# A two-layer decoder trunk on one core: GpSimd's instructions in the order in which the program emits them

## The chip, the cores and the metric

The kernel runs on one core of a Trainium2 chip. The metric is the device time of one execution in microseconds, lower is better; before the change it was run three times. The profile shows one further execution of the same program.

## The reference

Two layers, each with x of 512 tokens by 1024 channels, all in float32:

```
h = rms_norm(x) ; proj = h @ w_in[l]
pool_u, rq, rk, rv, rg, xq, gates = split(proj)
y_pool = pool_mixer(pool_u) ; y_ret = retention(rq, rk, rv, rg) ; y_mem = memory_attention(xq, rms_norm(mem))
merged = sum over branches of sigmoid(gate_b) * (y_b @ w_up_b)
x = x + merged @ w_out[l]
x = x + square(relu(rms_norm(x) @ w_mlp1[l])) @ w_mlp2[l]     # 1024 -> 4096 -> 1024
```

After the two layers a last rms_norm is returned.

## The kernel before, in words

A float32 product is made of float32r parts: `split` and `split_w` turn a tile into a high part (a ScalarE cast, L104 for operands, L114 for weights) and a low part (a VectorE subtraction, L105 and L117), and `mm` (L120 to L125) issues three matmuls, high by high (L123), high by low and low by high.

Most weights are multiplied as a `Weight`: a block of 1024 by 1024 in four quarters q00, q01, q10, q11, and seven products in the order 1, 2, 5, 3, 6, 4, 7, instead of eight. A weight has three raw operands of two tiles each (kp = 0 and 1, 512 KB a tile), loaded by the SyncE queue (L200): A from q00, C from q10, B from q11. Each tile serves several products, because the sums are formed in place by accumulating transfers that GpSimd issues (`take`, L222 on), always after the split of the value that is replaced:

- product 1 splits A, then A += q01 (L236, from DRAM); product 5 splits that, then A += q11 (L236); product 6 splits that, with nothing added.
- product 3 splits B, then B += q01 (L236); product 7 splits that.
- product 2 splits C; when product 6 has split A, C += A (L238, from SBUF to SBUF); product 4 splits that.

In the text A0 and A1 are A's tiles for kp 0 and 1, and likewise B0, B1, C0 and C1. `skip` (L217 to L219) does the first of these sums for a weight whose product 1 was made ahead from a separate copy (`early`). So GpSimd has eight transfers for a weight, emitted as A0, A1 (+q01), A0, A1 (+q11), B0, B1, C0, C1:

```
            raw = self.buf[part][kp]
            wp = split_w(raw, between)
            if then is not None:
                nc.gpsimd.dma_start(raw, rows2(then, kp), accum_op=ALU.add)
            if p == 6:
                nc.gpsimd.dma_start(self.buf["C"][kp], raw, accum_op=ALU.add)
```

GpSimd has one other task: the power -1/2 of each norm's mean square (`rstd`, L555 to L557): `r` for the norms over a layer's rows, `yss` for the four token blocks of a retention head pair, `mr` for the memory's norm.

The operand of a product (`Operand`) has its own sums and splits x1 to x7; for a weight whose operand was used before they are there already, for the first weight of an operand they are made beside the weight's splits.

Splits are prepared ahead of their products: `push` (L176) queues a product with its preparation, and `prepare` runs the preparations of the LOOK = 3 products ahead (2 for product 4). Per layer the weights follow one another like this: five projection weights (retention values; retention queries and keys; the gates of three branches), the memory's keys and values (a `Plain` weight without products of sums), the retention gate, memory queries with pool channels, three `Plain` weights for the branches, w_out, then for each of four blocks the MLP's first (w_mlp1) and second product (w_mlp2). The second products add into x.

Two things decide the order of the instructions on an engine. For engines named in `MANUAL` (L37, handed to `tc.manual_schedule` at L78) it is the order in which the program emits them; that is TensorE. For all others a scheduler chooses an order from the dependences and priorities before the kernel runs; once chosen, it is fixed. The transfers of SyncE's queue, too, are in such an order.

Of the kernel before, what the change touches and what calls it, by code (L numbers as in the profile page):

```python
# [16 lines left out]
ET = mybir.EngineType  # L17
# [16 lines left out]
MAGIC = 12582912.0  # L34
NSLOT = 72
LOOK = 3
MANUAL = {ET.PE}  # L37


C_CNT = 0  # L40
# [28 lines left out]
def tile_trunk(ctx, tc, a, out):  # L69
# [7 lines left out]
    psum = ctx.enter_context(tc.tile_pool(name="psum", bufs=8, space=PSUM))  # L77
    ctx.enter_context(tc.manual_schedule(engines=MANUAL))  # L78

# [1218 lines left out]
```

## Time and profile before

| | us |
|---|---|
| three runs | 1693.96, 1690.39, 1689.86 |
| median | 1690.39 |
| the profiled execution, its own time | 1696.11 |
| its span, first to last instruction | 1694.4 |
| TensorE busy | 1619.8 (96%) |
| VectorE busy | 1263.5 (75%) |
| ScalarE busy | 1034.9 (61%) |
| GpSimd busy | 313.5 (19%) |

PE is TensorE, DVE VectorE, ACT ScalarE, POOL GpSimd. The busy share says how much of the span an engine computed; for GpSimd it holds the issuing of its transfers, not their flight. The granted clock of TensorE was 0.983 of full speed on average. In the rows, "idle before <-releaser" is the time for which an engine stood still before an instruction, and what ended that. A transfer that adds into a raw tile reads as raw<-in_w_... (from DRAM) or raw<-raw (L238).

### The profile page before, as it was taken

The numbers are of one execution on the slowest core, as the hardware profiler recorded it, in microseconds if no ns is written. First come the engines' busy times: TensorE is split into PE (matmuls) and PEld (weight loads), VectorE is DVE, ScalarE is ACT, GpSimd is POOL, SyncE is SP. The second block draws the span as 40 slices with busy tenths as digits, with TensorE's granted clock in tenths as the row PEclk, the third lists the DMA queues.
The fourth block names the chain that finished last, engine by engine and source line by source line (L and its number), as shares of the span: only waits on it lengthen the run. The fifth ranks groups of instructions, "written<-read, shape, count | busy, mean of one in ns | idle before, by whom it ended". The sixth has DMA issues, their size and how long they took to land. (4 is left out here: it accounts for less than half of the span.)

```text
span 1694.4 us, 24933 instructions
## 1 busy us (share of the span) xinstructions
PE 1619.8 (96%) x9396; PEld 1425.3 (84%) x9396; DVE 1263.5 (75%) x1727; ACT 1034.9 (61%) x1655; POOL 313.5 (19%) x292
## 2 busy tenths in 40 slices
PE   8899999999989899999989999999999889999997
PEld 7697888998879788989768888889878688989895
DVE  4787575767687788696966876757767778796868
ACT  6456676556357656475765577755544577566565
POOL 2122212200012222222231223022000212222221
PEclk9999999999999899999999999999999999999999
DMA  8699986873666788988887999678435769788775
GB/s 237 148 237 234 252 217 142 186 223 118 181 137 133 153 198 178 213 179 202 183 182 162 234 248 243 217 169 175 158 125 159 173 153 192 189 181 185 174 151 123
DMA packets 155256, 311.16 MB, mean 184 GB/s; under 512 B 11320, under 2 KB 12544, under 8 KB 155136
## 3 DMA queue, kind: packets, MB, share of 16 engines
q0 software_dynamic: 61440, 134.23, 46.3%
q1 hardware_dynamic: 83872, 159.42, 27.5%
q10 hardware_dynamic: 9824, 15.93, 2.6%
q8 instruction: 73, 1.20, 0.3%
q14 instruction: 47, 0.39, 0.1%
HBM read 255.01 MB, written 16.78 MB: 160 GB/s over the span
## 5 line engine op out<-in xcount | busy, mean ns | idle before, releaser
L117 DVE TENSOR_TENSOR wl<-raw,wh 128x1024 fp32r<-128x1024 f32 x496 | 603.7, 1221 | 291.4 <-ACT wh L114 282.0
L114 ACT CAST wh<-raw 128x1024 fp32r<-128x1024 f32 x496 | 519.5, 1051 | 487.7 <-PE P L125 126.6
L236 POOL DMA_DIRECT2D raw<-in_w_mlp x92 | 121.6, 1349 | 391.8 <-DVE wl L117 270.9
L236 POOL DMA_DIRECT2D raw<-in_w_in x80 | 104.9, 1371 | 355.1 <-DVE wl L117 209.9
L238 POOL DMA_DIRECT2D raw<-raw x64 | 57.6, 900 | 167.9 <-DMA raw<-in_w_in 68.6
L1184 DVE TENSOR_TENSOR x<-x,P 128x512 f32<-128x512 f32 x120 | 78.4, 679 | 5.1 <-PE P L125 4.9
L123 PE MATMUL P<-wh,x3h 128*128 128x512 f32 x160 | 64.4, 403 | 11.3 <-ACT x3h L104 11.3
L123 PE MATMUL P<-wh,x6h 128*128 128x512 f32 x160 | 64.6, 404 | 9.8 <-ACT x6h L104 6.5
L125 PE MATMUL P<-wh,x6l 128*128 128x512 f32 x160 | 64.4, 402 | 4.2 <-DVE x6l L105 4.2
L123 PE MATMUL P<-x6h,wh 128*128 128x256 f32 x192 | 56.6, 295 | 10.7 <-ACT P L368 10.7
L236 POOL DMA_DIRECT2D raw<-in_w_out x12 | 15.9, 1461 | 274.4 <-DVE wl L117 156.6
L125 PE MATMUL P<-wh,x5l 128*128 128x512 f32 x160 | 63.5, 397 | 2.8 <-DVE x5l L105 2.8
L123 PE MATMUL P<-wh,x5h 128*128 128x512 f32 x160 | 63.3, 396 | 2.0 <-ACT x5h L104 1.9
L124 PE MATMUL P<-wl,x4h 128*128 128x512 f32 x160 | 62.7, 392 | 2.3 <-DVE wl L117 2.3
L125 PE MATMUL P<-wh,x3l 128*128 128x512 f32 x160 | 64.3, 402 | 0.1
L124 PE MATMUL P<-wl,x6h 128*128 128x512 f32 x160 | 63.9, 399 | 0.0
L123 PE MATMUL P<-wh,x7h 128*128 128x512 f32 x160 | 63.5, 397 | 0.3
L124 PE MATMUL P<-wl,x3h 128*128 128x512 f32 x160 | 63.7, 398 | 0.0
L123 PE MATMUL P<-wh,x4h 128*128 128x512 f32 x160 | 62.8, 393 | 0.5 <-ACT wh L114 0.5
L123 PE MATMUL P<-wh,x1h 128*128 128x512 f32 x160 | 63.1, 395 | 0.0
L124 PE MATMUL P<-wl,x7h 128*128 128x512 f32 x160 | 62.6, 391 | 0.0
L124 PE MATMUL P<-wl,x1h 128*128 128x512 f32 x160 | 62.6, 391 | 0.0
(314 smaller groups left out, 5213.4 us busy)
## 6 DMA issues: line engine op xcount, KB each, us to landing
raw<-in_w_mlp SPq DMA_DIRECT2D x100, 512.0 KB, 5.0
raw<-in_w_mlp POOLq DMA_DIRECT2D x96, 512.0 KB, 7.3
raw<-in_w_in SPq DMA_DIRECT2D x88, 512.0 KB, 5.3
raw<-in_w_in POOLq DMA_DIRECT2D x84, 512.0 KB, 7.6
raw<-raw POOLq DMA_DIRECT2D x64, 512.0 KB, 6.7
sgl<-sig SPq DMA_DIRECT2D x48, 256.0 KB, 6.0
sig<-c ACTq DMA_DIRECT2D x36, 256.0 KB, 5.6
raw<-in_w_mem_kv SPq DMA_DIRECT2D x16, 512.0 KB, 5.4
```

Of the source, the lines that this page charges most:

```text
L114: nc.scalar.copy(hi, raw)
L117: nc.vector.tensor_tensor(lw, raw, hi.bitcast(F32), ALU.subtract)
L123: nc.tensor.matmul(ps, sh, mh, start=start, stop=False, skip_group_check=True)
L124: nc.tensor.matmul(ps, sh, ml, start=False, stop=False, skip_group_check=True)
L125: nc.tensor.matmul(ps, sl, mh, start=False, stop=stop, skip_group_check=True)
L236: nc.gpsimd.dma_start(raw, rows2(then, kp), accum_op=ALU.add)
L238: nc.gpsimd.dma_start(self.buf["C"][kp], raw, accum_op=ALU.add)
L1184: nc.vector.tensor_tensor(x, x, part, op)
```

## The change

GpSimd joins the engines whose instructions stay in the order of emission. How far ahead the splits are prepared (LOOK) stays as it was.

```
 NSLOT = 72
 LOOK = 3
-MANUAL = {ET.PE}
+MANUAL = {ET.PE, ET.Pool}
```

TensorE's and SyncE's instructions stand in the same order as before; GpSimd's change all along the program; ScalarE's and VectorE's change only at the borders of stages, as the scheduler that still orders them sees another GpSimd.

In the second product of the MLP's block 1 in layer 0, GpSimd's order was this (raw_6069 and raw_6071 are A0 and A1, raw_6383 and raw_6385 B0 and B1, raw_6255 and raw_6257 C0 and C1):

```order
L236 DMA raw_6069<-in_w_mlp2 128x2x512
L236 DMA raw_6071<-in_w_mlp2 128x2x512
L236 DMA raw_6069<-in_w_mlp2 128x2x512
L236 DMA raw_6071<-in_w_mlp2 128x2x512
L238 DMA raw_6255<-raw_6069 128x1024
L236 DMA raw_6383<-in_w_mlp2 128x2x512
L238 DMA raw_6257<-raw_6071 128x1024
L236 DMA raw_6385<-in_w_mlp2 128x2x512
```

and is this now:

```order
L236 DMA raw_6069<-in_w_mlp2 128x2x512
L236 DMA raw_6071<-in_w_mlp2 128x2x512
L236 DMA raw_6069<-in_w_mlp2 128x2x512
L236 DMA raw_6071<-in_w_mlp2 128x2x512
L236 DMA raw_6383<-in_w_mlp2 128x2x512
L236 DMA raw_6385<-in_w_mlp2 128x2x512
L238 DMA raw_6255<-raw_6069 128x1024
L238 DMA raw_6257<-raw_6071 128x1024
```

Both of B's sums moved ahead of both of C's.

At the start of layer 1, with its first projection weight (raw_8133 and raw_8135 are A0 and A1, raw_8407 and raw_8409 B0 and B1, raw_8317 and raw_8319 C0 and C1; raw_8609 and raw_8611 are the next weight's A0 and A1), GpSimd's order was:

```order
L236 DMA raw_8133<-in_w_in 128x2x512
L557 TENSOR_TENSOR r_8381<-r_8381,nhalf_90 128x2
L236 DMA raw_8135<-in_w_in 128x2x512
L219 DMA raw_8609<-in_w_in 128x2x512
L557 TENSOR_TENSOR r_8507<-r_8507,nhalf_90 128x2
L219 DMA raw_8611<-in_w_in 128x2x512
L236 DMA raw_8133<-in_w_in 128x2x512
L238 DMA raw_8317<-raw_8133 128x1024
L236 DMA raw_8135<-in_w_in 128x2x512
L236 DMA raw_8407<-in_w_in 128x2x512
L238 DMA raw_8319<-raw_8135 128x1024
L236 DMA raw_8409<-in_w_in 128x2x512
```

and is now:

```order
L557 TENSOR_TENSOR r_8381<-r_8381,nhalf_90 128x2
L236 DMA raw_8133<-in_w_in 128x2x512
L236 DMA raw_8135<-in_w_in 128x2x512
L557 TENSOR_TENSOR r_8507<-r_8507,nhalf_90 128x2
L236 DMA raw_8133<-in_w_in 128x2x512
L236 DMA raw_8135<-in_w_in 128x2x512
L236 DMA raw_8407<-in_w_in 128x2x512
L236 DMA raw_8409<-in_w_in 128x2x512
L238 DMA raw_8317<-raw_8133 128x1024
L238 DMA raw_8319<-raw_8135 128x1024
L219 DMA raw_8609<-in_w_in 128x2x512
L219 DMA raw_8611<-in_w_in 128x2x512
```

The power of the first half's factors moved to the front, the next weight's skip sums to the end, and C0's sum no longer stands ahead of A1's second one.

In the last gate weight of layer 0 (C0 and C1 are raw_1765 and raw_1767, B0 and B1 raw_1869 and raw_1871) and at the start of the retention gate's weight (A0 and A1 are raw_2475 and raw_2477) it was:

```order
L238 DMA raw_1765<-raw_1565 128x1024
L238 DMA raw_1767<-raw_1567 128x1024
L236 DMA raw_1869<-in_w_in 128x2x512
L236 DMA raw_1871<-in_w_in 128x2x512
L557 TENSOR_TENSOR mr_2119<-mr_2119,nhalf_90 128x1
L557 TENSOR_TENSOR mr_2182<-mr_2182,nhalf_90 128x1
L236 DMA raw_2475<-in_w_in 128x2x512
L557 TENSOR_TENSOR yss_2674<-yss_2674,nhalf_90 128x2
L236 DMA raw_2477<-in_w_in 128x2x512
L557 TENSOR_TENSOR yss_2724<-yss_2724,nhalf_90 128x2
L557 TENSOR_TENSOR yss_2776<-yss_2776,nhalf_90 128x2
L557 TENSOR_TENSOR yss_2810<-yss_2810,nhalf_90 128x2
```

and is now:

```order
L236 DMA raw_1869<-in_w_in 128x2x512
L557 TENSOR_TENSOR mr_2119<-mr_2119,nhalf_90 128x1
L236 DMA raw_1871<-in_w_in 128x2x512
L238 DMA raw_1765<-raw_1565 128x1024
L557 TENSOR_TENSOR mr_2182<-mr_2182,nhalf_90 128x1
L238 DMA raw_1767<-raw_1567 128x1024
L557 TENSOR_TENSOR yss_2674<-yss_2674,nhalf_90 128x2
L557 TENSOR_TENSOR yss_2724<-yss_2724,nhalf_90 128x2
L557 TENSOR_TENSOR yss_2776<-yss_2776,nhalf_90 128x2
L557 TENSOR_TENSOR yss_2810<-yss_2810,nhalf_90 128x2
L236 DMA raw_2475<-in_w_in 128x2x512
L236 DMA raw_2477<-in_w_in 128x2x512
```

C's sums moved behind B's and between the two memory powers, and the retention gate's A sums behind the last of the four retention powers.

## Rows read from the trace of the kernel before

**Rows 1.** The page, busy time, share of the span and instructions of the engines.

```profile
PE 1619.8 (96%) x9396; PEld 1425.3 (84%) x9396; DVE 1263.5 (75%) x1727; ACT 1034.9 (61%) x1655; POOL 313.5 (19%) x292
```

**Rows 2.** TensorE's waits: waiting instruction, releaser, us in total, times, longest.

```profile
PE P L123 <- ACT P L368: 14.0, 4, 6.5
...
PE tr L454 <- ACT xn L586: 7.2, 4, 2.3
```

**Rows 3.** Timeline: start, us, instruction; GpSimd, then ScalarE, weight of memory queries.

```profile
325.85 3.69 POOL L236 DMA_DIRECT2D raw<-in_w_in  x3 [10.19 <-DVE wl L117]
...
334.61 0.86 POOL L238 DMA_DIRECT2D raw<-raw  x1 [1.68 <-DMA raw<-in_w_in]
...
342.64 1.05 ACT L114 CAST wh<-raw 128x1024 fp32r<-128x1024 f32 x1 [6.07 <-DMA raw<-raw]
...
345.18 2.00 ACT L114 CAST wh<-raw 128x1024 fp32r<-128x1024 f32 x2 [0.90 <-DMA raw<-raw]
```

**Rows 4.** MLP block 1: timelines of GpSimd and VectorE; landings of L238, L236 (+q11).

```profile
664.93 0.90 POOL L238 DMA_DIRECT2D raw<-raw  x1 [3.23 <-DMA raw<-in_w_mlp]
...
668.36 0.90 POOL L238 DMA_DIRECT2D raw<-raw  x1 [1.29 <-DMA raw<-in_w_mlp]
...
664.99 1.22 DVE L117 TENSOR_TENSOR wl<-raw,wh 128x1024 fp32r<-128x1024 f32 x1
...
DMA to landing us min/median/max: 5.6/6.9/8.1
...
DMA to landing us min/median/max: 6.5/7.0/7.6
```

**Rows 5.** The same block, timelines of ScalarE, VectorE and TensorE.

```profile
672.88 1.07 ACT L114 CAST wh<-raw 128x1024 fp32r<-128x1024 f32 x1
673.83 0.64 ACT L104 CAST x6h<-xs 128x512 fp32r<-128x512 f32 x1
676.58 2.09 ACT L114 CAST wh<-raw 128x1024 fp32r<-128x1024 f32 x2 [2.11 <-DMA raw<-raw]
...
675.17 1.22 DVE L117 TENSOR_TENSOR wl<-raw,wh 128x1024 fp32r<-128x1024 f32 x1
676.31 0.68 DVE L105 TENSOR_TENSOR x6l<-xs,x6h 128x512 fp32r<-128x512 f32 x1
...
677.42 0.39 PE L123 MATMUL P<-wh,x6h 128*128 128x512 f32 x1
```

**Rows 6.** Third projection weight, layer 0: timelines of GpSimd, ScalarE and TensorE.

```profile
133.80 0.90 POOL L238 DMA_DIRECT2D raw<-raw  x1 [2.28 <-DMA raw<-in_w_in]
...
137.35 1.05 ACT L114 CAST wh<-raw 128x1024 fp32r<-128x1024 f32 x1 [2.24 <-DMA raw<-raw]
...
142.68 1.05 ACT L114 CAST wh<-raw 128x1024 fp32r<-128x1024 f32 x1 [3.76 <-DMA raw<-raw]
...
145.04 0.50 PE L124 MATMUL P<-wl,x4h 128*128 128x512 f32 x1 [0.76 <-DVE wl L117]
```

**Rows 7.** Last gate weight of layer 0: timelines of GpSimd and ScalarE.

```profile
224.62 0.56 POOL L557 TENSOR_TENSOR mr<-mr,nhalf 128x1 f32<-128x1 f32 x1 [4.47 <-DVE mr L556]
...
224.06 1.03 ACT L114 CAST wh<-raw 128x1024 fp32r<-128x1024 f32 x1
```

**Rows 8.** The weight of the retention gate, layer 0: timeline of GpSimd.

```profile
279.72 0.69 POOL L557 TENSOR_TENSOR yss<-yss,nhalf 128x2 f32<-128x2 f32 x1 [1.88 <-DVE yss L556]
283.84 1.23 POOL L236 DMA_DIRECT2D raw<-in_w_in  x1 [3.43 <-DVE wl L117]
```

**Rows 9.** First projection weight of layer 1: timelines of GpSimd, ScalarE and TensorE.

```profile
847.67 1.20 POOL L236 DMA_DIRECT2D raw<-in_w_in  x1 [18.52 <-ACT wh L114]
...
877.35 0.90 POOL L238 DMA_DIRECT2D raw<-raw  x1 [8.30 <-DMA raw<-in_w_in]
...
885.74 1.99 ACT L114 CAST wh<-raw 128x1024 fp32r<-128x1024 f32 x2 [4.80 <-DMA raw<-in_w_in]
...
889.35 0.79 PE L123 MATMUL P<-wh,x3h 128*128 128x512 f32 x1 [4.67 <-ACT x3h L104]
```

## The prediction

> **What bounds the kernel now.** I read the busy shares first: TensorE is busy for 1619.8 of 1694.4 us [rows 1], so 74.6 us of the span are all that any order of GpSimd's instructions could give back, while a late operand costs its full delay as soon as it reaches TensorE. Next the waits of TensorE: the largest group ends with ScalarE's copies of P (14.0 us in 4 stalls), another with its scaling of xn by the norm's factors (7.2 us in 4) [rows 2]. Neither names GpSimd. GpSimd sits two steps behind: its accumulating transfers form A+q01, A+q11, B+q01 and C+A, whose landings release ScalarE's casts (L114), VectorE's subtractions (L117), and then the matmuls. So the places to read are those where a sum that lands later or earlier moves a split that TensorE is about to need.
>
> The price of a place in GpSimd's queue comes from the weight that holds the memory queries and pool channels, because its eight transfers already leave in the order that the change gives to all weights: A0, A1, A0, A1, B0, B1, then C0 and C1. Three of them leave from 325.85 on, and the sum in C1 as soon as A1's second sum has landed, at 334.61; ScalarE waits for C0 until 342.64 and for C1 until 345.18 [rows 3]. So after the landing of A's last sum it takes **8.0 us to C0 and 10.6 us to C1**: four transfers of 512 KB that follow one another 2.6 us apart. TensorE does not stall there, which is the first rival's evidence.
>
> **The MLP's second products (six of eight).** The first order excerpt shows the change: C0, B0, C1, B1 becomes B0, B1, C0, C1. In block 1 of layer 0, C0 goes at 664.93, when A0 has landed, and C1 at 668.36, when A1 has landed; they land 5.6 and 8.1 us later, at 670.5 and 676.5 [rows 4]. A1 does not move, because what is ahead of it does not. B1 is ready when VectorE's subtraction at 664.99 ends [rows 4], before A1's landing; so both B transfers stand ahead of C0. By the 8.0 and 10.6 us, C0 lands near 676.4 (5.9 later) and C1 near 679.0 (2.5 later).
>
> What meets it is ScalarE's order, which the change leaves as it is: the cast of C0 (672.88) stands ahead of the cast of x6's second half (673.83), and on VectorE C0's subtraction (675.17) ahead of x6's (676.31) [rows 5]. So x6, which needs nothing from GpSimd, is held up by C0: cast of C0 from 676.4 to 677.45, x6h to 678.1, subtraction of C0 to 678.7, x6l to 679.3. TensorE uses x6h at 677.42 and x6l two matmuls (0.45 us) later [rows 5]. The delay is 679.3 − 677.9 = 1.4 us with everything at its best, and 2.2 if the transfers follow each other 3 us apart as in rows 4 rather than 2.6; I take 2.0. Blocks 1 to 3 of both layers have this shape: 6 × 2.0 = **+12** (bounds: 0, if the scheduler's work behind it has room; 6 × 3.5 = 21 if C1's 2.5 us are paid too). In block 0 the skip sums of the next weight, which now go ahead of its own A sums, fall behind them, worth about what C loses: 0. Six of the MLP's first products (blocks 1 to 3) follow a second product whose end still occupies TensorE, with their x split long before: 0, and up to the same 2.0 each if that cover goes.
>
> **Projection weights whose C is late already.** In the third weight of layer 0, A1's landing lets C1 go at 133.80, ScalarE has stood idle 3.76 us for C1 when it lands at 142.68, and TensorE stalls for it at 145.04 [rows 6]. With both B transfers ahead, C1 lands at 133.8 + 10.6 = 144.4, 1.7 later, and C0 at 141.8. C0's cast begins at 137.35 now [rows 6], 4.4 earlier, less the 0.76 us of stall that is then already paid. So 1.7 to 3.6, and I take 2.4, nearer to C1's own shift, since the first of the two casts has some slack. The second weight of layer 0 and the third of layer 1 look the same: 3 × 2.4 = **+7** (bounds 3 and 13).
>
> **The gate weight and the one after it.** The third excerpt shows that B1 and C0 now stand behind the first `mr` power, and C1 behind the second. That second one waits 4.47 us for VectorE and runs at 224.62 [rows 7]. C0, behind B1, leaves near 221.7 and lands 5.6 to 8.1 later (the lengths of rows 4), at 227 to 230, where it is there in time today. ScalarE reaches C0's cast at 224.06 [rows 7], so it blocks 3 to 6 us, with the scores' and memory's splits queued behind. TensorE has other products queued; I take half, 3 us, in each layer: **+6** (bounds 0 and 10). In the weight for the retention gate, A's first sums now stand behind all four `yss` powers: behind that of 279.72 [rows 8], where the first sum goes ahead of them now. A+q11, issued at 283.84 now [rows 8], can go only when the sum issued at 280.4 has landed (6.5 us, as the first one of rows 4), been cast and subtracted (1.0 and 1.2 us, the casts and subtractions of rows 5): at 289.1, some 5 us later. Most of it is covered, since TensorE's next products of this stage come from elsewhere; I take 1.75 each, **+3.5** (bounds 0 and 8).
>
> **What is won.** In the first projection weight of layer 1, the second A+q11 goes only behind C0's sum, which keeps the engine idle for 8.30 us, until 877.35, for A0's landing. ScalarE waits 4.80 us for it at 885.74, and TensorE 4.67 us at 889.35 [rows 9]. In emission order it goes when its split is done, about 5 us earlier, and what is late next is C0, behind B's two; so 4.0 of the 4.67 are won here, and 3.0 in layer 0, whose first weight has the same rows. A's first sum holds GpSimd from 847.67 for 1.20 us [rows 9], and the power that gives the norm's factors, which stalls TensorE for xn [rows 2], stands behind it, as the second excerpt shows. It goes first now: −1.2 there, and the same at the two MLP norms. Together −4 − 3 − 3.6 = −10.6. What stands behind the power now is A's sum, under 1 us later and two products ahead of its use: 0. Everything else that moves (skip sums behind the previous weight's C1 in three places) has several weights' time until it is needed: 0, and if that cover went it would cost one transfer's 2.6 us each.
>
> **Sum.** 12 + 7 + 6 + 3.5 − 10.6 = +17.9 on the profiled execution's 1696.11 us (span 1694.4 and 1.7 around it). That execution lies 5.7 us above the median of the runs, 1690.39, so I set the forecast at 1690.4 + 17.9, rounded to **1708 us**. A measurement of this kernel tells about 0.3% (5 us) from no change, so "same" is 1685.3 to 1695.5.
>
> **Rivals.** *First, no change, 1691 us:* the late C is hidden, as in the weight of rows 3, where C arrives 8.0 us after A and TensorE does not stall. Then the +12 and the +9.5 of the gate stage shrink to some +5 together, the +7 remains, and −10.6 takes it back. For it: those rows. Against it: x6 behind C0 in ScalarE's queue [rows 5], which that weight lacks, since its operand was split long before. The spacing of transfers decides: under 2 us apart, C0 would land before 674.5 and x6 would be in time. The Trainium skill, "DMA: Bandwidth & Descriptors", section "Anatomy of one DMA — SWDGE (gpsimd) path", fits one such transfer as 2.0 us plus bytes over 436 GB/s, an estimate of 1.2 us for each further 512 KB if only the bytes follow one another. By that rule this rival would be the case; the 2.6 us of rows 3, for transfers that also add, speak against it.
>
> *Second, faster, about 1678 us:* one mechanism, the sum for C0 that today keeps GpSimd waiting for A0's landing while ready transfers stand behind it. It is gone in every weight. If the B sums that now leave up to 2.4 us earlier, and the A+q11 that no longer waits, bring every weight's splits forward as in the first, all the late terms are made up for, and −10.6 is left, with 1 or 2 us more at the stalls that end with ScalarE's copies of P [rows 2]. It decides if B's sum, not C's, is what ScalarE meets late. Against it: in the MLP the wait on record is for raw<-raw, C's sum [rows 5].
>
> *Third, much slower, about 1728 us:* the bounds above: C1's delay paid too in six products, 21, the projections 13, the gate weights 10 and the one after them 3.5; less 10.6: +37. It needs ScalarE's backlog to last until the seventh product.
>
> *Fourth, that order of emission moves nothing:* excluded, since the excerpts show GpSimd's order changed, and TensorE's the same.
>
> **Chances.** The forecast's case (from +6 to +28): 0.66; much slower, 0.11; no change, 0.13; faster, 0.10. So faster 0.10, same 0.13, slower 0.77. The range leaves out part of the two outer cases: 1686 to 1730; the forecast's own is 1696 to 1718.
>
> **What would show it.** Right: in the profile after, C0's cast in blocks 1 to 3 ends a wait of several us for raw<-raw, and TensorE has a new stall of 1.4 to 2.2 us for x6l at six places. The stall of 4.67 us for x3h is gone, the r power ahead of the first A sum. ScalarE waits longer for raw<-raw in the third projection weight. Wrong: no stall for x6 in the MLP, with C0 landing less than 6 us after A1 (then the first rival); or VectorE's and ScalarE's idle time growing without TensorE's (then the delays are covered).

## The result and the profile after

The change made the kernel slower: a median of 1751.88 us (1748.38 to 1754.94, 4 runs) against 1690.97 us for the kernel before (4 runs), a ratio of 1.0356 with a 95% interval of 1.0342 to 1.0369. That is 61 us, where 18 had been forecast, and outside the range. In the profiled executions the spans differ by 54.2 us (1748.6 against 1694.4). The other 6.7 us lie in the two executions: that of before was 5.1 us above its kernel's median, that of after (1750.39) 1.5 below its own.

The page of the changed kernel shows first the busy times of the engines, then the groups of lines 236 to 238 and of the weights' casts, and last a row of the table of transfers:

```profile
PE 1641.2 (94%) x9396; PEld 1434.3 (82%) x9396; DVE 1261.6 (72%) x1727; ACT 1033.9 (59%) x1655; POOL 315.0 (18%) x292
...
L114 ACT CAST wh<-raw 128x1024 fp32r<-128x1024 f32 x496 | 516.5, 1050 | 514.3 <-DMA raw<-raw 185.5
...
L238 POOL DMA_DIRECT2D raw<-raw x64 | 72.6, 1386 | 7.0 <-DMA raw<-in_w_in 6.9
...
raw<-raw POOLq DMA_DIRECT2D x64, 512.0 KB, 9.8
```

The same group of C's sums on the page before:

```profile
L238 POOL DMA_DIRECT2D raw<-raw x64 | 57.6, 900 | 167.9 <-DMA raw<-in_w_in 68.6
```

GpSimd no longer waits for A's landing ahead of C's sums: 7.0 us of such idle time in all 64 of them, where it was 167.9, because B's sums and their waits stand ahead. In return ScalarE waits 185.5 us for C's sums to land, where it waited 69.6. And TensorE's time grew in two ways against [rows 1]: the same 9396 matmuls are busy 21.4 us longer, and its idle time rose from 74.6 to 107.4 us.

TensorE's waits in the changed kernel (waiting instruction, releaser, us in total, times, longest), the first eight:

```profile
PE P L123 <- ACT P L368: 25.8, 4, 6.8
PE P L123 <- ACT x6h L104: 17.5, 10, 5.7
PE P L124 <- DVE wl L117: 8.7, 7, 2.2
PE P L123 <- ACT wh L114: 7.3, 4, 3.3
PE P L125 <- DVE x6l L105: 6.9, 8, 1.6
PE mtr L966 <- ACT mnf L969: 5.1, 2, 2.8
PE P L123 <- ACT x3h L104: 4.6, 3, 3.1
PE tr L454 <- ACT xn L586: 4.6, 3, 2.0
```

The group of P, 14.0 us in [rows 2], became 25.8, and x6h has ten stalls. Two of these waits shrank: that for x3h, and that for xn from 7.2 to 4.6 us, behind the power that now goes first. For x3h TensorE waited 11.3 us before:

```profile
PE P L123 <- ACT x3h L104: 11.3, 3, 5.8
```

TensorE's order is the same in all kernels of this text, so each matmul can be found again. The table takes the last matmul of product 7 in each weight, before TensorE turns to other work, and says by how much more its start in another kernel's profile lies behind that of before than it did one weight earlier. The last weight is taken to the end of the span. Summed by place, in us:

| place (both layers) | forecast | the change | pairs | pairs, later powers |
|---|---|---|---|---|
| first projection weight, with its r power | −8.2 | +1.3 | −6.5 | −4.5 |
| the next three projection weights | +7 | +7.7 | −1.4 | −2.4 |
| last gate weight | +6 | +11.7 | +15.3 | 0 |
| retention gate | +3.5 | +9.2 | +5.9 | +3.5 |
| memory queries and pool channels | 0 | 0 | 0 | 0 |
| w_out | 0 | +4.7 | −9.9 | −7.1 |
| MLP block 0, with its norm's r power | −2.4 | +1.2 | −6.3 | −6.1 |
| MLP blocks 1 to 3 | +12 | +18.5 | +0.1 | −0.1 |
| sum | +17.9 | +54.2 | −2.9 | −16.7 |

The last two columns are kernels of the next section. Each column is one execution, and a single figure is good to some us only: the same order in blocks 1 to 3 reads +18.5 here, +15.3 in the kernel m1 and +13.5 in the kernel e5 of the next section, and block 0, which the kernels m1, m2 and m3 leave alone, reads −3.2 to −1.7 in them.

In block 1 of layer 0, where the prediction was worked out, the changed kernel's timelines of GpSimd, ScalarE, VectorE and TensorE read:

```profile
680.35 1.20 POOL L236 DMA_DIRECT2D raw<-in_w_mlp  x1 [1.13 <-DVE wl L117]
...
686.42 1.20 POOL L236 DMA_DIRECT2D raw<-in_w_mlp  x1 [2.34 <-DVE wl L117]
687.15 2.30 POOL L238 DMA_DIRECT2D raw<-raw  x2
...
696.48 1.05 ACT L114 CAST wh<-raw 128x1024 fp32r<-128x1024 f32 x1 [3.59 <-DMA raw<-raw]
697.44 0.61 ACT L104 CAST x6h<-xs 128x512 fp32r<-128x512 f32 x1
...
697.56 1.22 DVE L117 TENSOR_TENSOR wl<-raw,wh 128x1024 fp32r<-128x1024 f32 x1 [2.43 <-ACT wh L114]
698.70 0.69 DVE L105 TENSOR_TENSOR x6l<-xs,x6h 128x512 fp32r<-128x512 f32 x1
...
698.10 0.50 PE L123 MATMUL P<-wh,x6h 128*128 128x512 f32 x1 [0.64 <-ACT x6h L104]
699.44 0.50 PE L125 MATMUL P<-wh,x6l 128*128 128x512 f32 x1 [0.62 <-DVE x6l L105]
```

This is [rows 5] with C late: A1's last sum is issued at 680.35 (660.50 in the trace of before), B1's at 686.42, C's two behind it. C0's cast waits for raw<-raw until 696.48, 16.1 us after A1's issue, where before C0 had landed 10.0 us after A1's issue; x6h follows it at once, VectorE keeps the same order, and TensorE stalls for x6h and then x6l.

### The profile page after: what moved, and what is told of

Same layout as the page of the kernel before. It is cut to its first block, busy times and chain, and to the rows that moved or that the text cites. A ratio compares the mean times of both kernels' runs of the same rounds, so it can differ in the third digit from the quotient of the medians.

```text
span 1748.6 us, 24988 instructions
## 1 busy us (share of the span) xinstructions
PE 1641.2 (94%) x9396; PEld 1434.3 (82%) x9396; DVE 1261.6 (72%) x1727; ACT 1033.9 (59%) x1655; POOL 315.0 (18%) x292
## 4 chain that ended last, share of the span: by engine, by line
issue 44%; PE 26%; DMA 16%; POOL 6%; DVE 4%; ACT 3%; POOLq 0%; SPq 0%; ACTq 0%; DVEq 0%
DMA raw<-in_w_mlp 6%; DMA raw<-raw 6%; PE P L124 5%; PE P L123 5%; PE P L125 5%; DMA raw<-in_w_in 4%; POOL raw L236 4%; POOL raw L238 2%; DVE wl L117 2%; ACT wh L114 1%; PE up L123 1%; PE up L124 1%; PE up L125 1%; PE kv L123 1%; PE kv L124 1%
## 5 line engine op out<-in xcount | busy, mean ns | idle before, releaser
L114 ACT CAST wh<-raw 128x1024 fp32r<-128x1024 f32 x496 | 516.5, 1050 | 514.3 <-DMA raw<-raw 185.5
L236 POOL DMA_DIRECT2D raw<-in_w_mlp x92 | 111.4, 1232 | 476.7 <-DVE wl L117 348.7
L236 POOL DMA_DIRECT2D raw<-in_w_in x80 | 97.5, 1258 | 345.9 <-DVE wl L117 283.1
L123 PE MATMUL P<-wh,x6h 128*128 128x512 f32 x160 | 69.1, 432 | 30.3 <-ACT x6h L104 17.5
L124 PE MATMUL P<-wl,x4h 128*128 128x512 f32 x160 | 67.8, 424 | 7.4 <-DVE wl L117 7.4
L123 PE MATMUL P<-wh,x4h 128*128 128x512 f32 x160 | 67.7, 423 | 7.3 <-ACT wh L114 7.3
L125 PE MATMUL P<-wh,x6l 128*128 128x512 f32 x160 | 68.1, 425 | 6.9 <-DVE x6l L105 6.9
L238 POOL DMA_DIRECT2D raw<-raw x64 | 72.6, 1386 | 7.0 <-DMA raw<-in_w_in 6.9
L123 PEld LDWEIGHTS P<-wh,x6h 128*128 128x128 f32 x160 | 32.8, 205 | 41.8 <-ACT x6h L104 21.7
L125 PE MATMUL P<-wh,x4l 128*128 128x512 f32 x160 | 66.1, 413 | 0.0
L236 POOL DMA_DIRECT2D raw<-in_w_out x12 | 14.5, 1209 | 283.3 <-DVE wl L117 283.3
```

The costliest lines, as they stand in the source:

```text
L114: nc.scalar.copy(hi, raw)
L123: nc.tensor.matmul(ps, sh, mh, start=start, stop=False, skip_group_check=True)
L124: nc.tensor.matmul(ps, sh, ml, start=False, stop=False, skip_group_check=True)
L125: nc.tensor.matmul(ps, sl, mh, start=False, stop=stop, skip_group_check=True)
```

## Experiments

The first three kernels put only a part of the program in order of emission, by a block around it. In the first and the third the other engines keep the order of before throughout; in the second ScalarE's and VectorE's order changes at a few places of these weights.

**The MLP alone** (label m1):

```
+            with tc.manual_schedule(engines=MANUAL | {ET.Pool} if c else MANUAL):
                 act = Operand(2)
...
```

> Order of emission for GpSimd only while blocks 1 to 3 of each layer's MLP are emitted; all other engines keep the order of before. Theory (C's sums behind B's hold up ScalarE's and VectorE's queues, some 2 to 3 us per second product, as summed over these blocks in the changed kernel's trace): 16 us slower than before, between 12 and 20, with TensorE's stalls for x6h and x6l in six products. Rival (the loss comes from the borders of stages, where powers and skip sums stand in line): within 4 us of before.

1711.56 us, ratio 1.0101 (1.0080 to 1.0121), 18.8 us over before's 1692.73. In the profile blocks 1 to 3 lose 15.3 us, by the table's measure. The theory's term holds, and the rival's is out.

**The last gate weight to the retention gate alone** (m2):

```
+        with tc.manual_schedule(engines=MANUAL | {ET.Pool}):
             products(hop, gate_done(0))
...
             products(hop, swish)
```

> Order of emission for GpSimd only from the last gate weight to the retention gate's weight of each layer. From the changed kernel's trace, by how much later these weights' products start: 17 us slower than before, between 12 and 22, if the pieces add up. Rival (these delays are only passed on from other weights, or are covered): 6 us or less.

1716.74 us, ratio 1.0139 (1.0122 to 1.0156): 24 us, above the expected 12 to 22. So these weights are late of themselves, not by what others pass on; by the table's measure the gate weights lose 11.5 us and the retention gates 10.2.

**The first four projection weights alone** (m3):

```
+        with tc.manual_schedule(engines=MANUAL | {ET.Pool}):
             products(hop, v_done, ahead=(1, True))
...
             products(hop, gate_done(2))
```

> Order of emission for GpSimd only for the first four projection weights of each layer. Theory (late C outweighs the freed second sum of A): 12 us slower than before, between 7 and 16. Rival, the prediction's own terms (7 lost, 7 to 8 won): within 3 us of before.

1708.70 us, ratio 1.0092 (1.0076 to 1.0107): 16 us, at the upper end of the expected 7 to 16. So the prediction's balance of this part (about zero) is wrong, with ScalarE's and VectorE's order as before. The three parts cost 18.8 + 24.0 + 16.0 = 58.8 us of the 61: they add up.

**The place of C's sums alone: pairs** (e1). The changed kernel, GpSimd still in order of emission, but with each half of B's sum emitted behind C's:

```
-            if then is not None:
+            if then is not None and p != 3:
                 nc.gpsimd.dma_start(raw, rows2(then, kp), accum_op=ALU.add)
             if p == 6:
                 nc.gpsimd.dma_start(self.buf["C"][kp], raw, accum_op=ALU.add)
+                nc.gpsimd.dma_start(self.buf["B"][kp], rows2(q(0, 1), kp), accum_op=ALU.add)
```

> The changed kernel, with each of B's sums issued behind C's sum of the same half: C0, B0, C1, B1 in every weight, GpSimd still in order of emission. Theory (place of C behind B): most of the loss goes, 1700 us, between 1688 and 1712; what is left is the gate stage, where C still stands behind the memory's powers. Rival (waiting in line as such, powers and skip sums, costs the time): 1735 us or more.

1694.66 us, ratio 1.0012 (1.0002 to 1.0023) to before. All other engines have exactly the changed kernel's order here, so by the two ratios (1.0356 and 1.0012) some 58 us of the change's 61 come from B's sums standing ahead of C's. Powers and skip sums stand in line as in the change. What is left to see is the gate weight; timelines of GpSimd, ScalarE and TensorE with the pairs:

```profile
221.43 0.56 POOL L558 TENSOR_TENSOR mr<-mr,nhalf 128x1 f32<-128x1 f32 x1 [2.27 <-DVE mr L557]
221.96 1.03 POOL L238 DMA_DIRECT2D raw<-raw  x1
...
229.16 1.99 ACT L114 CAST wh<-raw 128x1024 fp32r<-128x1024 f32 x2 [4.17 <-DMA raw<-raw]
...
235.48 1.11 PE L967 MATMUL mtr<-ident,mi 128*128 128x128 f32 x4 [6.14 <-ACT mnf L970]
```

C1's sum waits for the memory's power, ScalarE for C1, and TensorE for the memory's gains behind that cast.

**Pairs, with the memory's powers later** (e4): both powers and the scalings behind them are emitted after the gate weight's sums.

```
-                rstd(r, 1.0 / D)
-                for j in range(2):
-                    nc.vector.tensor_scalar_mul(mi[j], mi[j], r)
-                yield
-                yield
+                rs.append(r)
+                yield
+                if m == 0:
+                    yield
+            for m in range(NM):
+                rstd(rs[m], 1.0 / D)
+                for j in range(2):
+                    nc.vector.tensor_scalar_mul(mis[m][j], mis[m][j], rs[m])
+            yield
```

> The pairs of the run before (C0, B0, C1, B1), and both powers of the memory's norm emitted behind the gate weight's C1 and B1. Theory (in the gate weight it is the power ahead of C's sum, waiting for VectorE, that holds ScalarE at C1's cast and TensorE behind it, 6.7 and 6.6 us in the trace of the pairs): 1682 us, between 1677 and 1687, so faster than before. Rival (the memory's chain itself is what TensorE waits for, so that a later power only moves the stall): 1694 or more.

**1680.58 us**, ratio 0.9914 (0.9897 to 0.9930): faster than both kernels. The gate weight's 15.3 us are gone, as the theory said. ScalarE's and VectorE's order moved at a few places of this stage as well, so the 15.3 us are those of the edit as a whole.

**The changed kernel with the later powers only** (e5, the same edit without the pairs).

> The changed kernel (B0, B1, C0, C1) with only the memory's powers behind the gate weight's sums. Theory: C then leaves some 5 us earlier in that weight, but still behind both of B's; 5 to 10 us less than the changed kernel, 1744 us. Rival (powers in line cost most of the loss): 1725 or less.

1751.91 us, ratio 1.0335 (1.0315 to 1.0355), where the change had 1.0356: some 4 us less, and the intervals overlap. The theory's 5 to 10 us are not there. The gate weights lose 6.8 us instead of 11.7, but the retention gates 13.3 instead of 9.2. While C stands behind B in the next weight too, the time won in one seems to go back in the next; that is read from one profile and not shown further.

**C's sums both ahead of B's** (e6, on the pairs with late powers):

```
-                nc.gpsimd.dma_start(self.buf["B"][kp], rows2(q(0, 1), kp), accum_op=ALU.add)
+                for i in range(2 * kp):
+                    nc.gpsimd.dma_start(self.buf["B"][i], rows2(q(0, 1), i), accum_op=ALU.add)
```

> As the pairs with late powers, but both of C's sums ahead of both of B's: C0, C1, B0, B1, so that only the order of C1 and B0 differs. Theory (C's place decides, B's sums have two products' time): 1682 us, within 4 us of the pairs. Rival (the second of the two queues' heads is as costly: C1 waiting for A1's landing holds up B0): 8 us or more above the pairs.

1689.40 us, ratio 0.9968 (0.9950 to 0.9986): 8.8 us above the pairs with late powers, as the rival had it. C1's sum waits for A1 with B0's, ready, behind it. In the retention gate's weight TensorE then stalls at product 7, for a copy of c that stands behind B1's cast; timelines of ScalarE and TensorE:

```profile
310.31 1.04 ACT L114 CAST wh<-raw 128x1024 fp32r<-128x1024 f32 x1 [2.97 <-DMA raw<-in_w_in]
311.26 1.07 ACT L389 COPY c<-P 128x512 f32<-128x512 f32 x2
...
311.89 0.80 PE L123 MATMUL P<-wh,x7h 128*128 128x512 f32 x1 [3.30 <-ACT c L389]
```

By the table's measure the retention gates lose 9.2 us more than with the pairs and later powers, which is about the whole difference.

**Each pair turned round: B0, C0, B1, C1** (e9, on the same kernel; only GpSimd's order differs):

```
-            if then is not None and p != 3:
+            if then is not None and (p, kp) != (3, 1):
...
-                nc.gpsimd.dma_start(self.buf["B"][kp], rows2(q(0, 1), kp), accum_op=ALU.add)
+                if kp == 0:
+                    nc.gpsimd.dma_start(self.buf["B"][1], rows2(q(0, 1), 1), accum_op=ALU.add)
```

> The pairs with late powers, each pair turned round: B0, C0, B1, C1. C0 then stands behind one B instead of none (pairs) or two (the change); C1 stands last, as in the change. Theory (C0's lateness is what costs, since its cast stands ahead of x6's in ScalarE's queue; C1 has slack in the MLP): C0 lands some 3 us later than with the pairs, of which the MLP's second products cover all but 0.5 us each, and the third projection weights lose 1 to 2 us; 1690 us, between 1684 and 1700. Rival (C1 is as costly as C0, or each place costs the same): half of the loss or more, 1712 us or later.

1723.98 us, ratio 1.0171 (1.0150 to 1.0192). The theory falls, the rival holds: one place costs 43 us against the pairs' 1680.58, of some 71 that both places cost (1751.91). TensorE's largest wait is again that for P, as in the change. Behind it the waits for x6h have shrunk (17.5 us in the change) and those for the weights' low parts have grown (8.7 us there). The three here, and then the low parts in the pairs with late powers:

```profile
PE P L123 <- ACT P L370: 27.9, 4, 7.5
PE P L124 <- DVE wl L117: 12.6, 17, 2.0
...
PE P L123 <- ACT x6h L104: 4.2, 2, 2.2
```

```profile
PE P L124 <- DVE wl L117: 3.1, 4, 0.8
```

Seventeen stalls instead of four: nine at product 4, whose weights are C's, and six at product 7, whose split follows C1's. In MLP blocks 1 to 3, where C0 arrives nearly in time again and TensorE has no stall for x6, the loss is 7.3 us in all; both places cost 13.5 there (e5). So C1's place is about half of the matter in these blocks. Elsewhere this run moves C0 and C1 together, and does not tell their shares apart.

**The small loads of the first weight on another queue** (e7, on the changed kernel; e8, on the pairs with late powers). In layer 0's first weight ScalarE's own transfers were slow to issue in the changed kernel; its queue and engine, and TensorE:

```profile
56.12 5.36 ACTq L650 DMA_DIRECT2D posi<-in_positions  x2
61.52 0.62 ACT L104 CAST x6h<-xs 128x512 fp32r<-128x512 f32 x1 [8.99 <-DMA posi<-in_positions]
...
64.11 0.79 PE L123 MATMUL P<-wh,x6h 128*128 128x512 f32 x1 [6.08 <-ACT P L368]
```

Both edits:

```
-            nc.scalar.dma_start(pi[64 * j:64 * j + 64, :], a["positions"][:, j * HT:(j + 1) * HT].broadcast_to([64, HT]))
+            nc.sync.dma_start(pi[64 * j:64 * j + 64, :], a["positions"][:, j * HT:(j + 1) * HT].broadcast_to([64, HT]))
...
-            nc.scalar.dma_start(rest[o:o + src.shape[0], :], src)
+            nc.sync.dma_start(rest[o:o + src.shape[0], :], src)
```

> The changed kernel, with the small loads of gains and positions (6 transfers, once, in layer 0's first weight) issued by SyncE instead of ScalarE. Theory (their slow issue on ScalarE, 10.6 us in the changed kernel's trace against 2.9 before, holds x6's cast for 8.99 us there): the stall of 6.08 us for P at 64 us shrinks to 2 us or less, the first weight's product 4 starts 3 to 5 us earlier, total 1748 us. Rival (C's late cast alone holds x6): the stall stays above 5 us.

1754.88 us, no gain. The stall went from 6.08 to 4.24 us, between the theory's 2 and the rival's 5:

```profile
58.19 1.05 ACT L114 CAST wh<-raw 128x1024 fp32r<-128x1024 f32 x1 [5.05 <-PE P L125]
59.14 0.61 ACT L104 CAST x6h<-xs 128x512 fp32r<-128x512 f32 x1
...
62.35 0.79 PE L123 MATMUL P<-wh,x6h 128*128 128x512 f32 x1 [4.24 <-ACT P L368]
```

With the loads gone, the cast of C1, now ahead of x6's on ScalarE, waits for a buffer and holds x6 just as well. (The scheduler also moved ScalarE's and VectorE's order at this place, so the two runs differ in more than the queue.)

> The pairs with late memory powers, with the same small loads issued by SyncE. Theory: with the pairs ScalarE's issue is less slow there (5.1 us for the six), so 0 to 3 us less than the pairs with late powers, 1679 us. Rival (the weight loads that stand behind them on SyncE come late instead): 2 us or more slower than those.

1685.41 us, ratio 0.9951 (0.9939 to 0.9964): 4.8 us more than without the edit, as the rival had it. What exactly is late behind these loads was not followed further.

## Why the prediction was wrong

**Direction and mechanism were right.** C behind B is the cause: the pairs take back 58 of 61 us. The price of a place holds: in block 1 of layer 0 C0 landed 8.4 us and C1 10.8 us behind A1, where [rows 3] gave 8.0 and 10.6, and against A1 C0 landed 5.9 us later than before, as foretold. In blocks 1 and 2 of both layers TensorE has the two stalls that were worked out, for x6h and x6l.

**The MLP term** was +12 and measured +18.5 (18.8 by the times of m1). In blocks 1 and 2 the four second products lost 1.9 to 3.8 us each, where 2.0 was set. In block 3 it was 5.1 and 3.8. What was left out there is C1, which the prediction has 2.5 us late but prices only in its bound of 21: TensorE waits 2.16 us for C1's low part in product 4, where it waited 0.77 before, and its next matmuls take 0.63 us instead of 0.40. TensorE in block 3 of layer 0, changed:

```profile
870.22 0.50 PE L124 MATMUL P<-wl,x4h 128*128 128x512 f32 x1 [2.16 <-DVE wl L117]
...
871.17 0.63 PE L124 MATMUL P<-wl,x4h 128*128 128x512 f32 x1
```

**Later projection weights:** +7, measured +7.7, but in the third weight of each layer alone (4.0 and 3.7 us), not in three weights of 2.4 each. The second weight of layer 0 lost nothing, so this agreement is luck in part.

**The step that failed first is "what is won".** It set −4 and −3 for the first weights, for the stall of 4.67 us in [rows 9] and its twin. The stall for x3h did shrink, to 0.78 us in layer 1 and from 5.85 to 3.10 in layer 0. But the price of what is late next was put at under 1 us, and it ate the gain; the changed kernel's TensorE ten microseconds on, layer 1:

```profile
909.57 0.50 PE L123 MATMUL P<-wh,x3h 128*128 128x512 f32 x1 [0.78 <-ACT x3h L104]
...
919.58 0.80 PE L123 MATMUL P<-wh,x6h 128*128 128x512 f32 x1 [6.72 <-ACT P L368]
```

Copies of P and x6's low part stand behind C1's split there, as in the MLP x6 stands behind C0's. The stall that was 1.66 us there before is now 6.72, and its twin in layer 0 6.08. Measured +1.3 with the power, where −8.2 was set: 9.5 us of the miss. Layer 0 lost 4.5 us, layer 1 won 3.1.

That the freed sum is worth something is seen with the pairs, −6.5. The prediction also left out two places that have the same wait: in w_out and in MLP block 0 the kernel before issues A1's second sum only behind C0's, which waits for A0's landing. GpSimd in w_out of layer 0, before:

```profile
481.71 0.90 POOL L238 DMA_DIRECT2D raw<-raw  x1 [5.59 <-DMA raw<-in_w_out]
482.30 2.80 POOL L236 DMA_DIRECT2D raw<-in_w_out  x2
```

The pairs win 9.9 us in w_out and 6.3 in block 0 (where 2 or 3 of them may lie in the execution of before); the change, with C behind B, loses at both.

**The second is the cover that was taken for granted.** The gate weight and the retention gate, halved for cover, took 11.7 and 9.2 us where 6 and 3.5 were set. In the retention gate TensorE's stalls are at product 4, whose weights are C's (1.53 us in layer 0, 3.30 in layer 1); the prediction had priced A's sums. The memory-query weight, set at 0, lost nothing, as foretold. But w_out, also at 0, lost 4.7 us. Together 16.1 us, the largest part of the miss. In w_out the wait for x6h grew from 3.01 to 5.36 us behind a cast that waited 5.08 us; ScalarE and TensorE there:

```profile
512.04 1.04 ACT L114 CAST wh<-raw 128x1024 fp32r<-128x1024 f32 x1 [5.08 <-DMA raw<-raw]
...
515.14 0.80 PE L123 MATMUL P<-wh,x6h 128*128 128x512 f32 x1 [5.36 <-ACT x6h L104]
```

Block 0 of the MLP and its norm: +1.2 for −2.4. The power itself won 2.6 us of the 3.6, at xn (above). Together 9.5 + 11.4 (gates) + 4.7 (w_out) + 3.6 (block 0) + 6.5 (MLP) + 0.7 (projections) = 36.4, but for rounding the miss on the profiled execution.

**What the sum had no term for is the clock.** The mean granted clock is 0.971 after, 0.983 before. After a long stall TensorE's matmuls run at the lower of its two levels, 1.2 GHz, for some microseconds. Windows of the changed kernel behind the stall of 6.08 us at 64.11, and around the two stalls of 0.64 and 0.62 us in the MLP (us; PE, PEld, DVE, ACT, POOL; PEclk; DMA share; GB/s):

```profile
64.10:69.00 4.90, 4.89 (x12) 3.88 (x13) 4.14 (x10) 1.18 (x2) 0.00 (x0) 0.53 0.33 98
69.00:75.00 6.00, 6.00 (x29) 4.93 (x28) 4.92 (x10) 3.80 (x6) 0.00 (x0) 1.00 0.02 9
690.00:710.00 20.00, 18.75 (x81) 14.87 (x81) 16.87 (x23) 10.65 (x14) 0.05 (x1) 1.00 0.79 210
```

After 6 us of waiting TensorE gets 0.53 of its clock for 4.9 us, after 0.6 us the full one. An estimate from the two mean clocks: time at half clock is twice what is missing from 1, so 0.034 × 1694 = 58 us before and 0.058 × 1749 = 101 us after. The 43 us more at half speed cost 22 us, against 21.4 us more busy time for the same matmuls. So of the 54.2 us some 33 are waiting and some 21 are matmuls at the lower clock, and a long stall cost more than its length. The prediction's "a late operand costs its full delay" priced the waiting alone; the 21 us lie within the figures of the places above.

**The rivals.** "No change", by the transfers' spacing, is out. The Trainium skill's fit in "DMA: Bandwidth & Descriptors", section "Anatomy of one DMA — SWDGE (gpsimd) path", would have had it so with an estimated 1.2 us for each further 512 KB. The trace disagrees: in block 1 of layer 0 B0, B1, C0 and C1 landed 2.4 to 3.4 us apart. "Much slower" at 1728 was nearest; its reason, C1's delay, was paid in two of the six products, and most of the time went elsewhere. "Faster" rests on GpSimd no longer idling ahead of C's sum; that happened (167.9 us of such idle time became 7.0) and gained less than the late C cost.

## What to carry to other kernels

Moving one engine to order of emission reorders everything in its queue. Find which of the reordered instructions feeds one that stands *ahead of others* on an engine with a fixed order, and price everything queued behind that, at every place, not only where the pattern is steady. Order by who needs the result first and by when the inputs are there; here pairing C's half with B's half in the emission did both, and moving two small powers behind them made the fastest kernel of those here (1680.58 us). Add the matmuls that run at the lower clock after a long stall to the price of the stall.

## What was not expected of the hardware

In layer 0's first weight ScalarE issued its two small loads of positions in 5.36 us, from 56.12 on. Two accumulating transfers of 512 KB, the skip sums, were then under way (they landed at 57.5 and 62.0). The kernel before shows the same loads in its ScalarE queue:

```profile
56.73 1.17 ACTq L650 DMA_DIRECT2D posi<-in_positions  x2
```

That transfers under way slow the issue is a guess that the rows do not bear out: before, one was under way too (until 58.8), and with the pairs the same loads took 3.04 us with three under way. No run here separated the cause. The other surprise is the price of one place in the queue: B0, C0, B1, C1 and C0, B0, C1, B1 differ by one transfer's place in each half, some 2.6 us of landing by [rows 3], and by 43 us of the kernel.
